# Attention weights turned by VectorE block transposes and transfers within SBUF, with 512-column value products

## The chip, the core and the metric

The kernel runs on one core of a Trainium2 chip. A core has a matrix engine (TensorE, PE in the profile, with PEld for its weight loads), VectorE (DVE), ScalarE (ACT), GpSimd (POOL) and SyncE (SP, which here only issues transfers), and 16 DMA engines that all queues share. On chip, data lie in SBUF (128 partitions); TensorE writes to PSUM. The metric is the device time of one execution in microseconds (us); lower is better. Each engine takes its own instructions strictly in the order in which the built program has them, and waits at an instruction until what it needs is there.

## What is computed

One layer with two parallel branches over 512 tokens of width 2048. In the attention branch there are 8 query heads of width 128 and 2 key/value heads. Cut to what matters:

```python
h = rms_norm(x, norm_w)
proj = jnp.einsum('bsd,de->bse', h, w_in)
q, k, v, g_attn, xr, g_lru = jnp.split(proj, SPLITS, axis=-1)
# attention_group, after norm and rope of q and k; 8 heads, 512 queries, 512 keys
s = jnp.einsum('bkgqd,bksd->bkgqs', q, k_t) * scale
p = jax.nn.softmax(s, axis=-1)
attn = jnp.einsum('bkgqs,bksd->bkgqd', p, v_t)
# lru_group: conv, two gated linear scans
mixed = concat([rms_norm(attn, attn_norm_w) * silu(g_attn),
                rms_norm(lru, lru_norm_w) * silu(g_lru)])
return x + jnp.einsum('bse,ed->bsd', mixed, w_out)
```

The scores of a block come out with 128 queries on the partitions and 512 keys along the row, which is right for the softmax. The sum over keys needs the keys on the partitions, so each head's 512 by 512 weights have to be turned between the two products. All matrix products are made in three parts from a high and a low half of each operand (`mm3`, lines 147 to 150): high by high, high by low, low by high.

## The kernel before, in words

The stages follow each other: the projection of the LRU inputs (with x turned on the way), the LRU branch under further projections, the q, k, v projections, attention, then the gates and the output projection. The TensorE order is written by hand for the whole kernel (`manual_schedule(engines={PE})`, line 983). A long TensorE work that waits for little (`fill`, the projection of the gates in `gates()`, line 1090) is woven with the attention chain by `weave` (line 336): each `yield n` of the chain lets n pieces of the fill follow, a piece being six 128x512 products. The other engines and the transfer queue of SyncE are ordered, for this stage, by a planner when the program is built; weight loads are asked for early (`high_priority(AHEAD)`, line 217) and go through a ring of three SBUF places (`wring`). A load thus waits until the VectorE split that last read its place is done (line 213). The split halves of a weight tile have four places each (`wh`, `wl`, line 210), two tiles to a load.

The attention stage (`attention`, line 624) has 32 steps, four blocks of 128 queries for each of eight heads:

- `weights` (line 581): three score products into a PSUM bank (`mm`, four banks), the row maximum on VectorE (line 588), the exponential with its row sum on ScalarE (591), the reciprocal on VectorE (592), and the scaling by it on GpSimd (593).
- `turn_weights` (line 596), two steps later: four 128x128 TensorE transposes into a PSUM bank (line 600), the high half by ScalarE (602), the low half by VectorE (603).
- `values` (line 605), for two blocks at once, three steps after the second of them began: twelve products of 256 columns into a bank, a VectorE copy out of it (615), and once a head a square on ScalarE and its sum on GpSimd.
- `turned` (line 573): the queries of a later head are turned on TensorE (541) and split. Two heads are held.
- After each step, `yield STEPS` lets two pieces of fill go. One transfer of `last_sums` (line 765), which adds up blocks of w_out in DRAM for the output stage, is also put in: adds on GpSimd's queue (750), copies on SyncE's (747).

The gates of the LRU branch are applied in `gate` (line 648), which writes the silu of a gate to working tiles of the attention pool and multiplies by it on VectorE.

Of the kernel before, what the change touches and what calls it, by code (L numbers as in the profile page):

```python
# [10 lines left out]
F32 = mybir.dt.float32  # L11
# [5 lines left out]
P = 128  # L17
# [13 lines left out]


LRU_K2, LRU_B4 = 12, 9
ATT_K2, ATT_B4 = 9, 9


AHEAD = 600
# [5 lines left out]
WARM, WARM2 = 14, 5  # L43


STEPS = 2


H = 256


C_Q, C_K, C_GA, C_XR, C_GL = 0, 1024, 1536, 2560, 3584
# [6 lines left out]
def hybrid_kernel(  # L59
# [51 lines left out]
    def nm(s):  # L111
        cnt[0] += 1
        return f"{s}_{cnt[0]}"
# [1 line left out]
    def x2():  # L115
        return pools["xw"].tile([P, SEQ], F32R, tag="x2", bufs=32, name=nm("x2"))

    def work():
        return ("lru", LRU_K2, LRU_B4) if "lru" in pools else ("att", ATT_K2, ATT_B4)

    def k2(dt=F32, shape=(P, SEQ)):
        pool, n, _ = work()
        return pools[pool].tile(list(shape), dt, tag="k2", bufs=n, name=nm("k2"))

    def b4(dt=F32, shape=(P, 2, SEQ)):
        pool, _, n = work()
        return pools[pool].tile(list(shape), dt, tag="b4", bufs=n, name=nm("b4"))

    def ev(dt=F32):

# [441 lines left out]

    def turned(rot, h):

        q = b4(F32R)
        split_ps(turn(rot, h), q[:, 0, :], q[:, 1, :])
        return q[:, 0, :], q[:, 1, :]

    last_scale = [None]

    def weights(q, g, t):

        qh, ql = q
        tt = slice(t * P, (t + 1) * P)
        sc = mm()
        mm3(sc, qh[:, tt], ql[:, tt], kth[g], ktl[g], True, True)
        mx = pools["att"].tile([P, 1], F32, tag="mx", bufs=6, name=nm("mx"))
        nc.vector.tensor_reduce(mx, sc, axis=AX.X, op=ALU.max, negate=True)  # L588
        p = k2()
        sm = pools["att"].tile([P, 1], F32, tag="sm", bufs=6, name=nm("sm"))  # L590
        nc.scalar.activation(p, sc, AF.Exp, bias=mx, accum_out=sm)
        nc.vector.reciprocal(sm, sm)
        last_scale[0] = nc.gpsimd.tensor_scalar(p, p, sm, 0.0, op0=ALU.mult, op1=ALU.add).ins
        return p

    def turn_weights(p, t, pth, ptl):
        tt = slice(t % 2 * P, (t % 2 + 1) * P)
        pt = mm()
        for s in range(NT):
            nc.tensor.transpose(pt[:, s * P : (s + 1) * P], p[:, s * P : (s + 1) * P], ident)  # L600
# [4 lines left out]
    def values(h, half, pth, ptl):  # L605

        gs = slice(h // G * HD, (h // G + 1) * HD)
        o = mm()[:, : 2 * P]
        for s in range(NT):
            mm3(o, vh[s][:, gs], vl[s][:, gs], pth[:, s, :], ptl[:, s, :], s == 0, s == NT - 1)  # L610
        if half == 0 and h % 2 == 0:
            ap_[h // 2] = aring.tile([P, 2, SEQ], F32, name=nm("av"))
        av, asum = ap_[h // 2][:, h % 2, :], sums["a"]
        to = slice(half * 2 * P, (half + 1) * 2 * P)
        nc.vector.tensor_copy(av[:, to], o)
        if half == 1:
            if h == 0:
                nc.scalar.activation(asum, av, AF.Square)
            else:
                sq = k2()  # L620
                nc.scalar.activation(sq, av, AF.Square)
                nc.gpsimd.tensor_add(asum, asum, sq)
# [24 lines left out]

    def gate(gs, pairs, row, sig):

        for e, g in enumerate(gs):  # L650
            if e == 0 or sig is not k2:
                ss = [sig() for _ in gs] if sig is k2 else [sig()]
                for s, src in zip(ss, gs if sig is k2 else [g]):
                    nc.scalar.activation(s, src, AF.Silu)
            s = ss[e] if sig is k2 else ss[0]
# [434 lines left out]
    def gates():  # L1090
        todo = iter(())
        for n, (c0, row) in enumerate(((C_GL, R_LN), (C_GL + SEQ, R_LN + 4), (C_GA, R_AN))):
# [6 lines left out]
                wait -= 1  # L1099
                yield  # L1100
            if n < 2:
                todo = gate(evac_bc(acc), hp[2 * n : 2 * n + 2], row, k2)
            else:
                late.extend(evac_bc(acc))

# [121 lines left out]
```

## Time and profile before

| | |
|---|---|
| median of 3 runs | 654.27 us (654.11 to 654.38) |
| span of the profiled execution | 652.6 us, 8664 instructions |
| attention stage (first to last row maximum on VectorE) | 275.4 to 417.9 us |
| TensorE busy | 646.9 us, 99% |
| VectorE, ScalarE, GpSimd busy | 475.7, 341.4, 101.2 us |

Only the span of the profiled execution is recorded. Beside the median of the unprofiled runs it leaves some 1.7 us for what lies around the span. In the profile, "busy" counts an instruction from its start to its modelled end; matmuls are pipelined, so a 128x512 product that shows 389 ns can be followed by the next after 227 ns. What a product costs is therefore read from the distance between starts, or from the chain of work that ended last, which gives each piece only the time by which it moved the end. A row of the timeline has the start in us, the duration in us, the engine, the line in the code and the operation, and in brackets how long the engine had stood idle before it and who released it.

### The profile page before, as it was taken

The page shows a single profiled execution, that of the slowest core. Times are in us where ns is not written, and L with a number is a line of the kernel's source. Part 1 is how long each engine was busy: PE and PEld are TensorE (multiplying, and loading weights), DVE is VectorE, ACT ScalarE, POOL GpSimd, SP SyncE. Part 2 cuts the span into 40 slices and gives each one's busy share as a digit, 9 for nine tenths or more (in the row PEclk, how much of TensorE's full clock was granted, in tenths as well). Part 3 has the DMA queues.
Part 4 walks back from the last instruction along what each step waited for, and adds up shares of the span by engine and source line. Part 5 has one row for each costly group of instructions (what it writes and reads, how often), then busy time and mean ns, then how long its engine had stood idle before and what let it go on. Part 6 is the DMA issues. An engine that isn't in the chain of part 4 may idle for free.

```text
span 652.6 us, 8664 instructions
## 1 busy us (share of the span) xinstructions
PE 646.9 (99%) x3059; PEld 538.9 (83%) x3059; DVE 475.7 (73%) x780; ACT 341.4 (52%) x598; POOL 101.2 (16%) x137
## 2 busy tenths in 40 slices
PE   9999999999999999999999999999999999999997
PEld 7888888888888888888888888888888888888885
DVE  5889689977688953855856567579837867797785
ACT  3534899489856515454744437454434554444441
POOL 0000101112013302142222434300000001020010
PEclk9999999999999999999999999999999999999999
DMA  9854685856468331467422575532336585798262
GB/s 291 281 143 127 142 207 152 207 139 152 140 198 255 100 93 33 124 129 187 109 66 54 123 128 115 91 105 74 116 101 204 180 292 179 283 318 274 76 194 96
DMA packets 56316, 102.48 MB, mean 157 GB/s; under 512 B 4696, under 2 KB 15056, under 8 KB 56272
## 3 DMA queue, kind: packets, MB, share of 16 engines
q1 hardware_dynamic: 48240, 84.09, 40.4%
q0 software_dynamic: 7712, 17.31, 15.6%
q10 hardware_dynamic: 320, 0.53, 0.3%
q8 instruction: 24, 0.39, 0.2%
q14 instruction: 20, 0.16, 0.1%
HBM read 97.71 MB, written 25.17 MB: 188 GB/s over the span
## 4 chain that ended last, share of the span: by engine, by line
PE 99%; DVE 0%; DVEq 0%; issue 0%; POOL 0%; POOLq 0%
PE pj L148 20%; PE pj L150 20%; PE pj L149 20%; PE mm L874 13%; PE pj L874 10%; PE mm L148 3%; PE mm L150 3%; PE mm L149 3%; PE mm L600 2%; PE mm L238 1%; PE pj L304 1%; PE mm L541 1%; PE mm L990 1%; PE mm L667 0%; PE mm L284 0%; DVE cb L905 0%
## 5 line engine op out<-in xcount | busy, mean ns | idle before, releaser
L148 PE MATMUL pj<-x,wh 128*128 128x512 f32 x376 | 149.1, 396 | 0.0
L150 PE MATMUL pj<-x,wl 128*128 128x512 f32 x376 | 147.0, 391 | 0.0
L149 PE MATMUL pj<-x,wh 128*128 128x512 f32 x376 | 146.4, 389 | 0.0
L212 ACT CAST wh<-wr 128x512 fp32r<-128x512 f32 x143 | 86.1, 618 | 80.3 <-PE pj L149 31.0
L213 DVE TENSOR_TENSOR wl<-wr,wh 128x512 fp32r<-128x512 f32 x144 | 101.6, 728 | 33.7 <-ACT wh L212 25.5
L725 ACT CAST wh<-wr 128x1024 fp32r<-128x1024 f32 (+1 forms) x72 | 60.6, 860 | 75.2 <-PE mm L874 37.2
L726 DVE TENSOR_TENSOR wl<-wr,wh 128x1024 fp32r<-128x1024 f32 (+1 forms) x72 | 68.6, 984 | 25.3 <-ACT wh L725 25.1
L150 PEld LDWEIGHTS pj<-x,wl 128*128 128x128 f32 x376 | 70.6, 188 | 15.2
L149 PEld LDWEIGHTS pj<-x,wh 128*128 128x128 f32 x376 | 70.7, 188 | 13.6
L148 PEld LDWEIGHTS pj<-x,wh 128*128 128x128 f32 x376 | 70.6, 188 | 13.3
L148 PE MATMUL pj<-wh,x 128*128 128x512 f32 x192 | 74.9, 390 | 0.0
L150 PE MATMUL pj<-wh,x 128*128 128x512 f32 x192 | 74.7, 389 | 0.0
L149 PE MATMUL pj<-wl,x 128*128 128x512 f32 x192 | 74.7, 389 | 0.0
L602 ACT CAST b<-mm 128x512 fp32r<-128x512 f32 x32 | 18.8, 586 | 62.2 <-PE mm L600 62.2
L874 PE MATMUL mm<-wh,ml 128*128 128x512 f32 x128 | 49.8, 389 | 0.0
L874 PE MATMUL mm<-wh,mh 128*128 128x512 f32 x128 | 49.8, 389 | 0.0
L874 PE MATMUL mm<-wl,mh 128*128 128x512 f32 x128 | 49.8, 389 | 0.0
L750 POOL DMA_DIRECT2D t<-in_w_out_dram x40 | 33.1, 838 | 102.0 <-DMA t<-in_w_out_dram 101.8
L588 DVE TENSOR_REDUCE mx<-mm 128x1 f32<-128x512 f32 x32 | 22.1, 690 | 33.4 <-PE mm L150 32.6
L150 PEld LDWEIGHTS pj<-wh,x 128*128 128x128 f32 x192 | 36.0, 188 | 7.6
L148 PEld LDWEIGHTS pj<-wh,x 128*128 128x128 f32 x192 | 36.1, 188 | 7.4
L149 PEld LDWEIGHTS pj<-wl,x 128*128 128x128 f32 x192 | 36.1, 188 | 7.3
(205 smaller groups left out, 1115.8 us busy)
## 6 DMA issues: line engine op xcount, KB each, us to landing
wr<-in_w_in_dram SPq DMA_DIRECT2D x71, 512.0 KB, 3.9
wr<-in_w_out_dram SPq DMA_DIRECT2D x24, 512.0 KB, 4.9
t<-in_w_out_dram POOLq DMA_DIRECT2D x40, 256.0 KB, 5.8
wr<-t SPq DMA_DIRECT2D x40, 256.0 KB, 4.2
t<-in_w_out_dram SPq DMA_DIRECT2D x24, 256.0 KB, 4.8
t<-t SPq DMA_DIRECT2D x16, 256.0 KB, 4.0
wr<-in_w_out_dram SPq DMA_DIRECT2D x16, 256.0 KB, 5.1
wr<-in_x_dram POOLq DMA_DIRECT2D x8, 512.0 KB, 5.8
```

The source lines that it names most:

```text
L148: nc.tensor.matmul(acc, lh, rh, start=start, stop=False)
L149: nc.tensor.matmul(acc, lh, rl, start=False, stop=False)
L150: nc.tensor.matmul(acc, ll, rh, start=False, stop=stop)
L212: copy(hi, raw[:, k, :])
L213: nc.vector.tensor_sub(lo, raw[:, k, :], f(hi))
L588: nc.vector.tensor_reduce(mx, sc, axis=AX.X, op=ALU.max, negate=True)
L600: nc.tensor.transpose(pt[:, s * P : (s + 1) * P], p[:, s * P : (s + 1) * P], ident)
L602: nc.scalar.copy(pth[:, :, tt], p3)
L725: nc.scalar.copy(hi[:, to], b)
L726: nc.vector.tensor_sub(lo[:, to], b, f(hi[:, to]))
L750: nc.gpsimd.dma_start(dst, src, accum_op=ALU.add)
L874: nc.tensor.matmul(dst[s], lh[:, ts_], rh, start=i == 0 and j == 0, stop=i == 7 and j == 2)
```

## The change

Per head, instead of per two blocks:

- each scaled weight block is turned by a VectorE instruction that transposes every 32x32 square by itself (line 594 of the changed kernel), into a tile `u` (two of them);
- `moved` (596): after the fourth block, 16 transfers on SyncE's queue carry the squares of a head to their partitions, from `u` into one tile `pt`, in pieces of 512 bytes, 32 partitions and 64 KB a transfer (602); then ScalarE makes the high half and VectorE the low half in two instructions each of 128x1024 (607, 608), into one pair `ph`, `pl`;
- `values` (611) makes twelve products of 512 columns a head, and the copy out of the bank (620) puts the columns back in order. It stands directly behind the score products of the fourth block of the next head;
- the TensorE transposes and the PSUM banks they took are gone; one head's queries are turned ahead instead of two;
- the silu of a gate is written in place (line 658), so that the attention pool needs no tiles for it; the fill gets 13 + 36 x 2 pieces within the chain instead of 13 + 35 x 2, and the rest follows as before.

```diff
-    def weights(q, g, t):
+    def weights(q, g, t, turned_):
...
         last_scale[0] = nc.gpsimd.tensor_scalar(p, p, sm, 0.0, op0=ALU.mult, op1=ALU.add).ins
-        return p
-
-    def turn_weights(p, t, pth, ptl):
-        tt = slice(t % 2 * P, (t % 2 + 1) * P)
-        pt = mm()
+        nc.vector.transpose(turned_[:, :, t, :], p)
+
+    def moved(turned_):
+
+        u = turned_.rearrange("p (s a) t c -> p a s (t c)", a=NQ)
+        pt = at("pt", 1, (NT, NQ, P))
+        for i in range(NQ):
+            for a in range(NQ):
+                nc.sync.dma_start(pt[a * B : (a + 1) * B, :, i, :], u[i * B : (i + 1) * B, a])
+        hi, lo = at("ph", 1, (NT, SEQ), F32R), at("pl", 1, (NT, SEQ), F32R)
+        p = pt.rearrange("p s i x -> p s (i x)")
+        for s in range(0, NT, 2):
+            ss = slice(s, s + 2)
+            nc.scalar.copy(hi[:, ss], p[:, ss])
+            nc.vector.tensor_sub(lo[:, ss], p[:, ss], f(hi[:, ss]))
+        return hi, lo
+
+    def values(h, hi, lo):
+
+        gs = slice(h // G * HD, (h // G + 1) * HD)
+        o = mm()
         for s in range(NT):
-            nc.tensor.transpose(pt[:, s * P : (s + 1) * P], p[:, s * P : (s + 1) * P], ident)
-        p3 = pt.rearrange("p (s q) -> p s q", q=P)
-        nc.scalar.copy(pth[:, :, tt], p3)
-        nc.vector.tensor_sub(ptl[:, :, tt], p3, f(pth[:, :, tt]))
...
-            mm3(o, vh[s][:, gs], vl[s][:, gs], pth[:, s, :], ptl[:, s, :], s == 0, s == NT - 1)
+            mm3(o, vh[s][:, gs], vl[s][:, gs], hi[:, s], lo[:, s], s == 0, s == NT - 1)
...
-        nc.vector.tensor_copy(av[:, to], o)
+        nc.vector.tensor_copy(
+            av.rearrange("p (t i c) -> p i t c", i=NQ, c=B),
+            o.rearrange("p (i t c) -> p i t c", i=NQ, c=B),
+        )
...
-        qs, ps_, pts = {h: turned(rots[0], h) for h in range(2)}, {}, {}
-        yield 13
+        qs, pts = {h: turned(rots[0], h) for h in range(1)}, {}
+        yield BEGIN
         last = NH * NT
-        for i in range(last + 3):
+        for i in range(last + NT):
             h, t = divmod(i, NT)
             if i < last:
-                ps_[i] = weights(qs[h], h // G, t)
+                if t == 0:
+                    u = at("u", 2, (SEQ // B, NT, B))
+                weights(qs[h], h // G, t, u)
                 next(transfers, None)
-                if t == 0 and h + 2 < NH:
-                    qs[h + 2] = turned(rots[(h + 2) // G], (h + 2) % G)
-            j = i - 2
-            if 0 <= j < last:
-                h, t = divmod(j, NT)
-                if t % 2 == 0:
-                    pts[j // 2] = b4(F32R, (P, NT, 2 * P)), b4(F32R, (P, NT, 2 * P))
-                turn_weights(ps_.pop(j), t, *pts[j // 2])
-            j = i - 3
-            if j >= 0 and j % 2 == 1:
-                values(j // NT, j // 2 % 2, *pts.pop(j // 2))
+                if t == 0 and h + 1 < NH:
+                    qs[h + 1] = turned(rots[(h + 1) // G], (h + 1) % G)
+                if t == NT - 1:
+                    pts[h] = moved(u)
+            if t == NT - 1 and h:
+                values(h - 1, *pts.pop(h - 1))
             yield STEPS
...
-            if e == 0 or sig is not k2:
-                ss = [sig() for _ in gs] if sig is k2 else [sig()]
-                for s, src in zip(ss, gs if sig is k2 else [g]):
+            if e == 0 or sig:
+                ss = [sig()] if sig else gs
+                for s, src in zip(ss, [g] if sig else gs):
                     nc.scalar.activation(s, src, AF.Silu)
```

More of the change, by code (lines that the diff above doesn't have):

```diff
@@ L43 @@
 WARM, WARM2 = 14, 5
-STEPS = 2
+BEGIN, STEPS = 13, 2
 H = 256
+B = 32
+NQ = P // B
 C_Q, C_K, C_GA, C_XR, C_GL = 0, 1024, 1536, 2560, 3584
@@ L116, in x2, with at @@
         return pools["xw"].tile([P, SEQ], F32R, tag="x2", bufs=32, name=nm("x2"))
-    def work():
-        return ("lru", LRU_K2, LRU_B4) if "lru" in pools else ("att", ATT_K2, ATT_B4)
     def k2(dt=F32, shape=(P, SEQ)):
-        pool, n, _ = work()
-        return pools[pool].tile(list(shape), dt, tag="k2", bufs=n, name=nm("k2"))
+        return pools["lru"].tile(list(shape), dt, tag="k2", bufs=LRU_K2, name=nm("k2"))
     def b4(dt=F32, shape=(P, 2, SEQ)):
-        pool, _, n = work()
-        return pools[pool].tile(list(shape), dt, tag="b4", bufs=n, name=nm("b4"))
+        return pools["lru"].tile(list(shape), dt, tag="b4", bufs=LRU_B4, name=nm("b4"))
+    def at(tag, bufs, shape, dt=F32):
+        return pools["att"].tile([P, *shape], dt, tag=tag, bufs=bufs, name=nm(tag))
     def ev(dt=F32):
@@ L586, in weights @@
         mm3(sc, qh[:, tt], ql[:, tt], kth[g], ktl[g], True, True)
-        mx = pools["att"].tile([P, 1], F32, tag="mx", bufs=6, name=nm("mx"))
+        mx, sm = (at(n, 6, (1,)) for n in ("mx", "sm"))
         nc.vector.tensor_reduce(mx, sc, axis=AX.X, op=ALU.max, negate=True)
-        p = k2()
-        sm = pools["att"].tile([P, 1], F32, tag="sm", bufs=6, name=nm("sm"))
+        p = at("p", 3, (SEQ,))
         nc.scalar.activation(p, sc, AF.Exp, bias=mx, accum_out=sm)
@@ L605, in values @@
[L605 to L609, printed above, removed]
-            mm3(o, vh[s][:, gs], vl[s][:, gs], pth[:, s, :], ptl[:, s, :], s == 0, s == NT - 1)
-        if half == 0 and h % 2 == 0:
+        nc.vector.transpose(turned_[:, :, t, :], p)
[12 more added lines that the diff above has]
+        return hi, lo
@@ L1101, in gates @@
             if n < 2:
-                todo = gate(evac_bc(acc), hp[2 * n : 2 * n + 2], row, k2)
+                todo = gate(evac_bc(acc), hp[2 * n : 2 * n + 2], row, None)
             else:
```

20 lines of the change are left out of this document (9 added, 11 removed).

## The prediction

> **What bounds the kernel now.** I read the page first (busy shares, then the chain that ended last), then the chain in order of time inside the attention stage, then the timeline of one attention step, then SyncE's waits and the transfer table, and last the granted clock.
>
> ```profile
> span 652.6 us, 8664 instructions
> PE 646.9 (99%) x3059; PEld 538.9 (83%) x3059; DVE 475.7 (73%) x780; ACT 341.4 (52%) x598; POOL 101.2 (16%) x137
> PE 99%; DVE 0%; DVEq 0%; issue 0%; POOL 0%; POOLq 0%
> ```
>
> TensorE is never without work: the chain is TensorE for 99% of the span. So what leaves TensorE's program shortens the kernel one for one, and every wait that is put into that program lengthens it one for one. Here is the attention stage on that chain (start, time on the chain, what):
>
> ```profile
> 299.99 0.24 PE mm L150
> 300.23 0.44 PE mm L600 x4
> 300.67 0.12 PE mm L148
> 300.78 0.12 PE mm L149
> ...
> 301.97 0.12 PE mm L150
> 302.08 0.23 PE pj L148
> ```
>
> Four turns cost 0.44 us, the twelve value products of 256 columns 302.08 - 300.67 = 1.41 us, and a 512-column product 0.23 us (0.227 in long rows).
>
> **What leaves TensorE.** The line of the turns, and the copy that stands once behind each set of value products:
>
> ```profile
> L600 PE MATMUL mm<-ident,k x128: 270/272/273, 282.6 to 425.8; 128*128 128x128 f32 x128
> L615 DVE COPY av<-mm x16: 404/416/426, 293.4 to 430.3; 128x256 f32<-128x256 f32 x16
> ```
>
> 128 turns are 32 groups: 32 x 0.44 = 14.1 us. Value products: 16 x 1.41 = 22.6 us become 8 x 12 x 0.227 = 21.8 us, so 0.8 us. The turns of the queries stay eight. Together 14.9 us off TensorE, if nothing waits.
>
> **What is added, and the wait it brings.** The changed kernel's built order decides here. For heads 2 and 3 it has (numbers tell tiles apart; u_3194 is head 3, pl_3149 and ph_3148 are head 2):
>
> ```
> TensorE   mm_3289 <- kt, q        three score products, head 3, fourth block
>           mm_3325 <- ph_3148      value products of head 2: high half
>           mm_3325 <- pl_3149      low half, the second of the twelve
> VectorE   mx_3293 (maximum), sm_3294 (reciprocal), u_3194 <- p_3296 (turn)   head 3, fourth block
>           pl_3149 <- pt_3131, ph_3148   twice, head 2
>           av_3338 <- mm_3325
> ```
>
> On TensorE the value products of head 2 stand directly behind the last scores of head 3. On VectorE their low half stands behind the turn of the block made from those same scores. So the second value product cannot start before scores, maximum, exponential, reciprocal, scaling, turn and split have run one after the other, and TensorE has nothing else to take. This is so at seven places (heads 0 to 6); at head 1 the low half stands behind the turn of the third block and the maximum of the fourth instead. One step of before gives the links:
>
> ```profile
> 299.83 0.40 PE L150 MATMUL mm<-kt,b 128*128 128x512 f32 x1
> 300.27 0.69 DVE L588 TENSOR_REDUCE mx<-mm 128x1 f32<-128x512 f32 x1
> 301.19 0.69 ACT L591 ACTIVATE k<-mm,mx 128x512 f32<-128x512 f32 x1
> 301.77 0.20 ACT L591 ACTIVATION_READ_ACCUMULATOR k<-mm,mx 128x1 f32 x1
> 302.00 0.16 DVE L592 RECIPROCAL sm<-sm 128x1 f32<-128x1 f32 x1
> 302.26 0.69 POOL L593 TENSOR_SCALAR k<-k,sm 128x512 f32<-128x512 f32 x1 [1.86 <-DVE sm L592]
> L726 DVE TENSOR_TENSOR wl<-wr,wh 128x1024 fp32r<-128x1024 f32 x40 | 48.6, 1223 | 20.0 <-ACT wh L725 19.8
> L725 ACT CAST wh<-wr 128x1024 fp32r<-128x1024 f32 x40 | 41.7, 1052 | 60.7 <-PE mm L874 35.6 <-DVE wr L827 11.1 <-PE pj L874 4.0
> ```
>
> From the start of the last score product: the maximum starts at 0.44 and ends at 1.13; the exponential can follow at 1.19 (here it came later, ScalarE was busy); from its start to the end of the scaling are 302.95 - 301.19 = 1.76, so 2.95. The turn has no row. Below it I put the 128x256 copy (0.42), above it the 128x1024 subtraction (1.22); I take 0.69, VectorE's 128x512 maximum, the same shape and type: 0.08 to start, 3.72. The first low half (128x1024 in SBUF, as line 726): 0.06 + 1.22, 5.00; TensorE goes on at 5.05. Unhindered, the second value product would start after two products, at 0.46. The wait is 4.6 us (4.3 to 5.1 with the ends for the turn). The second low half takes 1.2 us more and is hidden by the six products of the first (1.36 us). ScalarE's high half (1.05 us) runs while VectorE and GpSimd finish the block. VectorE itself gains per head four turns (2.8 us) and loses little; in
>
> ```profile
> 305.00:325.00 20.00, 20.00 (x113) 17.08 (x112) 15.63 (x28) 13.18 (x25) 3.91 (x6) 1.00 0.53 136
> 325.00:345.00 20.00, 20.00 (x111) 17.03 (x110) 11.74 (x22) 9.42 (x21) 5.02 (x6) 1.00 0.18 54
> ```
>
> (stretch; sum; then PE, PEld, DVE, ACT, POOL, clock, DMA share, GB/s) it is busy 15.6 and 11.7 of 20 us; a head will last over 21 us, so its amount of work isn't the bound, its order is. The weight splits behind the values (next chunk) are needed three fill pieces and more later, 4 us; hidden.
>
> [...]
>
> **The transfers.** They have one head's time, less what precedes. Rows:
>
> ```profile
> SPq L201 <- DVE wl L213: 309.1, 53, 12.9
> wr<-in_w_in_dram SPq DMA_DIRECT2D x71, 512.0 KB, 3.9
> k<-in_lru_wa_dram SPq DMA_DIRECT2D x8, 128.0 KB, 3.8
> k<-in_lru_wx_dram SPq DMA_DIRECT2D x8, 128.0 KB, 4.8
> 42.51 2.00 SPq L393 DMA_DIRECT2D k<-in_lru_wa_dram  x4
> 44.55 2.00 SPq L394 DMA_DIRECT2D k<-in_lru_wx_dram  x4
> DMA to landing us min/median/max: 3.6/4.8/6.1
> out_dram<-cb SPq DMA_DIRECT2D x3, 256.0 KB, 2.5
> out_dram<-cb POOLq DMA_DIRECT2D x4, 256.0 KB, 8.3
> L750 POOL DMA_DIRECT2D t<-in_w_out_dram x40 | 33.1, 838 | 102.0 <-DMA t<-in_w_out_dram 101.8
> ```
>
> An issue takes 0.5 us, and loads in 512-byte pieces (those of the LRU gate maps, eight of 128 KB: 1 MB, as much as a head's weights) land 3.8 to 4.8 us after it, at most 6.1. The 16 transfers of head 2 cannot start before the split of head 1 has left `pt`, which is when TensorE goes on at values 1 (time 0 now). In SyncE's order two weight loads stand among them (four, a load, six, a load, four), and a weight load waits until VectorE has split the tile that held its place: SyncE waits for that 309 us in all today, up to 12.9 us at once, and the last four transfers will wait behind it. The second load's place comes free after value products (2.5), two fill pieces (2.7), scores and turn (1.1), two pieces (2.7), scores (0.7), one piece (1.4), a cast (0.6), and a low half behind the reciprocal (1.3) that shares VectorE: 13.4 with the links' gaps. Four issues later, 15.3, plus 3.8 landing: 19.1; high half 1.1, low half 1.3, TensorE at 21.6. The chain of the fourth block ends at 16.9 us of TensorE work (4 x 0.7 scores, 0.44, 8 x 1.36, 2.7) plus 4.6, at 21.5. The two are even. If the transfers land 1 us later (4.8), each wait is 1 us longer; at 6.1, 2.3 us. If they land at 2.5, the lower end, from the fastest row of this queue above, the block's chain decides and nothing is gained. I take 4.8 us a wait: 7 x 4.8 = 33.6 us.
>
> Head 7 has no scores beside it: from values 6 TensorE has 2.5 + 8 x 1.36 = 13.4 us, and two loads stand among its transfers too, the second free at about 6.6; four issues and 3.8 land at 12.4, with both halves 14.8: 1 us of wait (0 to 3).
>
> SBUF writes of 8 MB more share the 16 DMA engines, busy 0.53 and 0.18 of those stretches: the weight loads, issued some 10 us ahead, cover that; uncovered, it is inside the 2.3 us above. The adds on GpSimd follow the scaling as before (0.8 us between blocks 3.4 us apart). Gates in place: the same instructions, free of charge; the tiles are in time, as a gate's projection takes over 60 us.
>
> **The clock.** A TensorE that stands still for over 4 us is something this trace shows only at its end:
>
> ```profile
> 1.13 3.17 PE mm L990 x14
> 5.56 1.07 PE mm L990 x5
> 6.62 1.17 PE pj L304 x4
> 647.59 0.39 PE L874 MATMUL mm<-wh,ml 128*128 128x512 f32 x1
> 650.00:651.00 1.00, 0.00 (x0) 0.00 (x0) 0.00 (x0) 0.00 (x0) 0.00 (x0) 1.00 0.43 128
> 651.00:652.00 1.00, 0.00 (x0) 0.00 (x0) 0.00 (x0) 0.00 (x0) 0.00 (x0) 0.96 0.00 0
> 652.00:652.60 0.60, 0.00 (x0) 0.00 (x0) 0.00 (x0) 0.00 (x0) 0.00 (x0) 0.50 0.00 0
> ```
>
> The granted clock (the third number from the right) falls to half at 651.92, 3.9 us after the last product ended. At the start (the first three rows, of the chain) a product of 256 columns takes 3.17 / 14 = 0.226 us, twice the 0.12 us above: half speed after standing still. Those at 5.56 still take 0.21; the four of 512 columns from 6.62 take 0.29 each, between 0.23 and its double, so full speed came back near 6.8, some 5.7 us after the first product. So gaps of 4.4 us (TensorE's first value product, with the high half, runs before the wait) may halve the clock in some heads. I take two of seven, since the gap is little longer than the 3.9 us, and 5.7 us at half rate after each, half of it lost: 2 x 2.8 = 5.7 us; ends 0 and 7 x 2.8 = 20 us. [...]
>
> **The sum.** -14.9 + 33.6 + 1 + 5.7 = +25.4 us. The profiled span of 652.6 leaves 1.7 us around it to the median of 654.27; both carry over. 654.3 + 25.4 = 679.7.
>
> **Rivals.**
> - Nothing waits (the other side): the low half of a head is ready before the scores of the next end, as its transfers would allow only if VectorE held it ahead of the fourth block's turn. 654.3 - 14.9 = 639.4. It decides where the wait falls under 14.9 / 7 = 2.1 us; maximum, exponential, scaling and split alone are 3.3. For it speaks only that TensorE's amount falls. 0.03.
> - The clock never falls: the gaps stay too short for it, as only one is seen to do so. 654.3 - 14.9 + 34.6 = 674. 0.24.
> - The clock falls in every gap: 654.3 - 14.9 + 34.6 + 20 = 694; for it speaks that the one gap seen did. 0.16.
> - The transfers are the bound: 32 partitions at a time, SBUF at both ends, no row shows it. At the 8.3 us of the outputs on GpSimd's queue the wait is 4.7 + 8.3 - 3.8 = 9.2 us: 654.3 - 14.9 + 64 + 4 (head 7), and with the clock down in each gap 20 more: 727. Against it: 512-byte pieces landed in 3.8. 0.12.
>
> **How the numbers follow.** My forecast has 0.45. Predicted 679.7. Range 668 (waits of 4.2 us, no clock fall) to 702 (waits of 5.5, all clocks): it holds the first, third and fourth case and leaves out some 0.2. A difference under 0.2% (1.3 us) cannot be told here; faster 0.03, same 0.01, slower 0.96.
>
> **What would show it.** TensorE idle in seven places of 4 to 6 us between 300 and 450 us, just ahead of products that read `pl`, released by VectorE's low half; no line of turns by `ident` on the weights; VectorE's turn near 0.69 us; the last transfer of a head landing close to the end of the next head's scaling; granted clock 1.00, or 0.50 behind some gaps. The prediction is wrong if VectorE's low half runs before the fourth turn, if the waits are released by transfers and far longer, or if TensorE also waits for weight splits (`wl`).

## The result and the profile after

The changed kernel takes 706.92 us (705.73 to 707.14) against 654.19 us beside it: 1.080 times as long, 95% interval 1.0785 to 1.0816. The forecast had 679.7 us, range 668 to 702: slower, as forecast, but by 52.7 us where 25.4 were given.

The page of the changed kernel: the span, busy shares, and the rows of TensorE's busy tenths and granted clock over 40 slices of 17.6 us.

```profile
span 704.9 us, 8366 instructions
PE 654.6 (93%) x2835; PEld 533.0 (76%) x2835; DVE 493.1 (70%) x788; ACT 346.0 (49%) x586; POOL 101.3 (14%) x137
...
PE   9999999999999999938977877797999999999997
...
PEclk9999999999999999969888978989999999999999
...
PE 77%; issue 6%; DMA 6%; DVE 4%; POOL 3%; ACT 2%; SPq 1%; DVEq 0%; ACTq 0%; POOLq 0%
```

TensorE was 99% of the chain before and is 77% now, and its holes lie in the attention slices alone (the last slice is the program's end), as do the clock's digits under 9. Who ended the holes, from the changed kernel's waits (us in total, times, longest):

```profile
PE mm L149 <- ACT ph L607: 38.2, 8, 11.5
PE mm L150 <- DVE pl L608: 6.3, 8, 1.4
```

That is 44.5 us in eight places. What the clock took is in the same kernel's windows, one for each stretch at half rate (length, TensorE busy, four other engines, clock, DMA share, GB/s):

```profile
303.18:316.83 13.65, 5.09 (x11) 3.71 (x12) 2.36 (x2) 1.99 (x2) 0.02 (x1) 0.50 0.79 215
...
357.79:364.61 6.82, 5.72 (x13) 4.15 (x14) 2.95 (x3) 0.89 (x1) 0.00 (x0) 0.50 0.16 39
...
sum 61.44, PE 40.27 PEld 29.45 DVE 22.38 ACT 11.47 POOL 4.73; mean PE 5.03 PEld 3.68 DVE 2.80 ACT 1.43 POOL 0.59
```

Eight stretches, one behind each gap, in which TensorE worked 40.3 us at half rate; at full rate, taking the granted 0.50 for half the pace, that is 20.1 us less (a product follows the one before after 0.43 us at 385.62 to 388.18, after 0.23 at 389.95 to 391.54). So: -14.9 (work that left TensorE) + 44.5 + 20.1 = 49.7 of the 52.3 us by which the span grew. The other 2.6 us lie in TensorE's work: at full rate it is 634.5 us (654.6 - 20.1), which is 12.4 less than the 646.9 of before, not 14.9.

Where a head's time goes shows on SyncE's timeline for the transfers of head 3, counted from 0 (start, length of the run of issues, line), and then on all engines where the fourth block of head 4 meets the value products of head 3:

```profile
360.78 4.45 SPq L602 DMA_DIRECT2D pt<-u  x7
368.34 0.37 SPq L202 DMA_DIRECT2D wr<-in_w_in_dram  x1
368.76 5.10 SPq L602 DMA_DIRECT2D pt<-u  x8
375.50 0.37 SPq L202 DMA_DIRECT2D wr<-in_w_in_dram  x1
375.92 0.59 SPq L602 DMA_DIRECT2D pt<-u  x1
```

```profile
378.12 0.40 PE L149 MATMUL mm<-kt,q 128*128 128x512 f32 x1
...
381.74 0.71 DVE L594 STREAM_TRANSPOSE u<-p 128x512 f32<-128x512 f32 x1 [0.82 <-POOL p L593]
382.25 1.99 ACT L607 CAST ph<-pt 128x1024 fp32r<-128x1024 f32 x2 [1.52 <-DMA pt<-u]
383.32 2.36 DVE L608 TENSOR_TENSOR pl<-pt,ph 128x1024 fp32r<-128x1024 f32 x2 [0.87 <-ACT ph L607]
383.34 0.79 PE L149 MATMUL mm<-ph,v 128*128 128x512 f32 x1 [4.35 <-ACT ph L607]
384.60 0.79 PE L150 MATMUL mm<-pl,v 128*128 128x512 f32 x1 [0.47 <-DVE pl L608]
```

The transfers' last landing (382.2) and the fourth block's turn (382.45) do end level. But the first value product waits too, for the high half, which needs only the transfers. (At heads 1 and 2 the high half follows the exponential on ScalarE without a pause, at 332.56 and 356.68 us, so there ScalarE's order ended the wait; at the other six it was a transfer.) And the transfers form a round: from 360.78, when the split of head 2 has left `pt`, 16 issues take 10.1 us, SyncE stands 3.1 and 1.6 us in front of two weight loads whose ring place is not free, and the 16th transfer lands late. Its time to landing is in the transfer table (last number, median), for the windows 360 to 368, 368.7 to 374.5 and 374 to 384 us:

```profile
pt<-u SPq DMA_DIRECT2D x7, 64.0 KB, 2.0
...
pt<-u SPq DMA_DIRECT2D x8, 64.0 KB, 3.4
...
pt<-u SPq DMA_DIRECT2D x1, 64.0 KB, 6.1
```

The median is 2.0 us for seven transfers with no load ahead and 3.4 for eight behind a 512 KB load and beside a w_out add; the one behind the second load, with two w_out adds beside it, took 6.1. (The first load had landed by then, at 372.6.) What makes the later ones slower these rows do not show; in a run below, with no load among the transfers, the medians of two heads are 2.0 us and, with w_out adds running among them, 3.8.

Head 0 is the worst, 12.0 us of waits. On SyncE's timeline, three copies for the output stage stand ahead of its transfers and wait for GpSimd's adds:

```profile
283.67 8.18 SPq L751 DMA_DIRECT2D t<-t  x3
...
292.53 8.17 SPq L602 DMA_DIRECT2D pt<-u  x8
...
301.38 5.87 SPq L602 DMA_DIRECT2D pt<-u  x8
```

### The profile page after: what moved, and what is told of

Its sections match the earlier page's. It is cut to its first block, busy times and chain, and to the rows that moved or that the text cites. A ratio compares the mean times of both kernels' runs of the same rounds, so it can differ in the third digit from the quotient of the medians.

```text
span 704.9 us, 8366 instructions
## 1 busy us (share of the span) xinstructions
PE 654.6 (93%) x2835; PEld 533.0 (76%) x2835; DVE 493.1 (70%) x788; ACT 346.0 (49%) x586; POOL 101.3 (14%) x137
## 4 chain that ended last, share of the span: by engine, by line
PE 77%; issue 6%; DMA 6%; DVE 4%; POOL 3%; ACT 2%; SPq 1%; DVEq 0%; ACTq 0%; POOLq 0%
PE pj L149 14%; PE pj L150 14%; PE pj L151 14%; PE mm L878 12%; PE pj L878 9%; PE mm L150 4%; PE mm L151 3%; PE mm L149 3%; DMA pt<-u 3%; DMA wr<-in_w_in_dram 2%; DVE pl L608 1%; POOL p L593 1%; PE mm L239 1%; DVE wl L214 1%; DMA t<-in_w_out_dram 1%
## 5 line engine op out<-in xcount | busy, mean ns | idle before, releaser
L214 DVE TENSOR_TENSOR wl<-wr,wh 128x512 fp32r<-128x512 f32 x144 | 103.2, 742 | 41.3 <-ACT wh L213 30.3
L149 PEld LDWEIGHTS pj<-x,wh 128*128 128x128 f32 x376 | 71.1, 189 | 14.8
L150 PEld LDWEIGHTS pj<-x,wh 128*128 128x128 f32 x376 | 71.0, 189 | 14.9
L151 PEld LDWEIGHTS pj<-x,wl 128*128 128x128 f32 x376 | 70.7, 188 | 15.1
L149 PE MATMUL mm<-ph,v 128*128 128x512 f32 x32 | 20.6, 645 | 38.2 <-ACT ph L607 38.2
L149 PEld LDWEIGHTS mm<-ph,v 128*128 128x128 f32 x32 | 9.9, 309 | 43.9 <-ACT ph L607 41.7
```

Of the source, the lines that this page charges most:

```text
L149: nc.tensor.matmul(acc, lh, rh, start=start, stop=False)
L150: nc.tensor.matmul(acc, lh, rl, start=False, stop=False)
L151: nc.tensor.matmul(acc, ll, rh, start=False, stop=stop)
L214: nc.vector.tensor_sub(lo, raw[:, k, :], f(hi))
```

## The experiments

All times are medians, with the ratio to the kernel before on the same chip. "High" and "low" are TensorE's waits for `ph` and `pl`, in us, in the profiled run; "half rate" is TensorE's busy time at a clock of 0.5. The profiled execution is one of those timed, and in two rows it lies well above the median: 673.9 us for 669.0 and 658.8 for 654.4. In the column of loads, "among" means that SyncE has weight loads between a head's transfers.

| run | tiles | values later by | loads | us | ratio (95%) | high, low | half rate |
|---|---|---|---|---|---|---|---|
| changed kernel | 1 | 0 | among | 706.9 | 1.080 (1.0785-1.0816) | 38.2, 6.3 | 40.3 |
| filler products | 1 | 0 | among | 700.3 | 1.071 (1.0677-1.0743) | 14.2, 5.3 | 15.2 |
| no transfers | - | 0 | - | 642.1 | 0.981 (0.9797-0.9826) | 0, 0 | 0 |
| halves first | 1 | 0 | among | 716.2 | 1.093 (1.0894-1.0956) | 49.0, 3.7 | 43.2 |
| values later | 1 | 1 | among | 705.0 | 1.077 (1.0754-1.0789) | 38.0, 5.3 | 40.7 |
| two queues | 1 | 0 | among | 687.3 | 1.050 (1.0478-1.0529) | 17.6, 6.4 | 32.3 |
| two tiles | 2 | 0 | among | 688.7 | 1.052 (1.0506-1.0542) | 35.1, 1.4 | 17.9 |
| two tiles, later | 2 | 1 | among | 682.0 | 1.041 (1.0384-1.0435) | 27.8, 0.9 | 20.5 |
| two tiles, later still | 2 | 2 | among | 669.0 | 1.023 (1.0173-1.0279) | 14.1, 3.7 | 26.0 |
| loads behind | 1 | 0 | behind | 684.9 | 1.045 (1.0427-1.0477) | 20.9, 8.0 | 26.9 |
| four wide transfers | 1 | 0 | among | 667.2 | 1.020 (1.0175-1.0221) | 15.1, 4.0 | 14.8 |
| later, two queues | 2 | 2 | among | 679.2 | 1.037 (1.0356-1.0391) | 7.9, 3.8 | 14.4 |
| later, loads behind | 2 | 2 | behind | 654.4 | 1.000 (0.9983-1.0013) | 5.1, 1.1 | 15.9 |
| one tile, later, loads behind | 1 | 1 | behind | 670.3 | 1.023 (1.0188-1.0272) | 10.4, 10.0 | 17.5 |

**Is the clock a cause of its own?** 34 products of 256 columns (put at 4.0 us, 3.7 in the trace) stand ahead of each head's value products, in the bank that these then clear.

```diff
         o = mm()
+        for _ in range(FILLER):
+            nc.tensor.matmul(o[:, : 2 * P], wv[:, :P], wv, start=True, stop=True)
```

> The changed kernel with 34 idle products of 128x256 (0.118 us each, 4.0 us in all) in front of each head's value products, into the same bank, so that TensorE stands still for less than 2 us at a time. Theory (the waits of 44.5 us in eight places halve the clock eight times, 40.3 us of work at half rate, 20 us lost): the clock stays at 1.00, the waits are filled but not shortened, about 687 us (685 to 693, since the shortest waits of 3.5 us are overfilled by half a us). Rival (the half clock costs nothing, as the transfers set the pace of a head): 707 us or a little more.

700.32 us. Work at half rate falls from 40.3 to 15.2 us, which is worth 12.5 us, but the time only by 6.6: what is left of the waits (19.5 us) and the 29.8 us of filler are 4.8 us more than the 44.5 us of waits before. TensorE at full speed reaches its wait sooner, and the transfers come when they come. The clock is part of the price, not its root.

**Are the transfers the root?** They are left out, and the halves made from the turned tile directly, so the weights are in the wrong rows.

```diff
-        for i in range(NQ):
-            for a in range(NQ):
-                nc.sync.dma_start(pt[...], u[...])
...
-        p = pt.rearrange("p s i x -> p s (i x)")
+        p = turned_.rearrange("p n t c -> p (n t c)").rearrange("p (s e) -> p s e", s=NT)
```

> The changed kernel without the 128 transfers: the halves are made from the tile that VectorE's turns have written, so the weights are in the wrong order and the value products are of other sums; all engines' work is the same. Theory (turns and splits on VectorE fit in, the wait comes with the transfers and the order they give): no waits, 639 to 642 us. Rival (VectorE's added turns or the one head's delay cost by themselves): over 650 us.

642.09 us, no wait for either half, clock full: the expectation holds. The turns, halves and 512-column products by themselves gain 12.3 us; the transfers cost 64.8.

**Is it the order on VectorE?** Once with the maximum and exponential of a fourth block ordered behind the halves of the head before, once with the value products a step (two fill pieces and a block of scores) later.

```diff
+        with behind(last_lo, t):
             nc.vector.tensor_reduce(mx, sc, axis=AX.X, op=ALU.max, negate=True)
...
+        with behind(last_hi, t):
             nc.scalar.activation(p, sc, AF.Exp, bias=mx, accum_out=sm)
```

> The changed kernel with one edit of order: on VectorE the maximum of a head's fourth block comes behind the low half of the head before, and on ScalarE its exponential behind the high half; so the halves no longer stand behind the fourth block's chain. Theory (two bounds that are about even, the chain of the fourth block and the transfers; the transfers of a head now begin one block's chain, some 3 us, later): waits as long or longer, now all released by transfers, 700 to 725 us. Rival (the order on VectorE alone makes the wait): waits fall to 1 us or less and the clock stays up, 642 to 652 us.

716.22 us, slower, as the theory had it: the halves wait for the transfers, and now the block waits behind the halves. Nearly all of its waits are for `ph` (49.0 us). Order alone is not the cause.

```diff
-BEGIN, STEPS = 13, 2
+BEGIN, STEPS = 11, 2
...
-            if t == NT - 1 and h:
-                values(h - 1, *pts.pop(h - 1))
+            hv, tv = divmod(i - 1, NT)
+            if tv == NT - 1 and hv > 0:
+                values(hv - 1, *pts.pop(hv - 1))
```

> The changed kernel with the value products one step (two pieces of fill, some 3.9 us with scores and a turn) later in TensorE's program. In the built order the low half again stands behind the turn of the block whose scores come just ahead of the value products. Theory (order): each wait stays near 4.2 us, the extra of the heads that waited for transfers (head 0: 7 us, heads 3, 4, 6: some 1 us, head 7: 4 us) goes, clock falls remain: 685 to 697 us. Rival (only the transfers are late): waits fall to under 1 us, 642 to 652 us.

704.99 us; both expectations fell. A step of work put in front of the value products bought next to nothing: head 0's wait fell from 12.0 to 8.0 us, and in sum the waits (38.0 and 5.3 us) are what they were. A round explains that. A head's halves begin when its transfers have landed, and the next head's transfers begin when these halves have left `pt`. In this run the low half of head 2 ended at 357.25, the transfers of head 3 began at 357.27 and the last of them landed at 378.90; head 3's high half began at 379.07, its low half ended at 382.51, and the next transfers began at 382.54. That is 25.3 us from start to start (24.9 in the changed kernel, 360.78 to 385.71), and the value products are no direct link of it (TensorE enters only through the weight loads among the transfers, which wait for a place). While the round is longer than TensorE's own work for a head, TensorE waits for the difference wherever they stand. The next runs take the round into their theories.

**Which link of the round?** First the issue: eight of a head's transfers go to ScalarE's queue. Then the tile: the low half is written over the transferred weights, and there are two such tiles, so that transfers need not wait for the split of the head before.

```diff
-                nc.sync.dma_start(pt[...], u[...])
+                (nc.sync, nc.scalar)[a % 2].dma_start(pt[...], u[...])
```

> Edit: of a head's 16 transfers eight are issued by ScalarE's queue and eight by SyncE's; one tile pt as in the changed kernel. Theory A (two bounds that stand level: the chain of the fourth block, and the round through the one tile pt): the transfers land some 4 us earlier (8 issues of 0.6 us less, weight loads in front of fewer), the chain of the fourth block stays, so the wait for the high half shrinks to under 2 us, that for the low half grows to 2 to 4 us, and the time is 692 to 706. Rival B (the round through pt alone sets the pace): every head is 4 to 5 us shorter, and with fewer falls of the clock 655 to 675. Rival C (what the transfers cost is their landing and the contention of the DMA engines, not their issue): nothing changes, 703 to 710.

687.34 us, between the two expectations: 20 us off, so issue and what stands between the issues weigh far more than "level" allows, and less than all. A new wait comes with it, 4.6 us for `p`: the exponentials queue behind ScalarE's issues.

```diff
-        pt = at("pt", 1, (NT, NQ, P))
+        pl = at("pl", 2, (NT, NQ, P), F32R)
+        pt = f(pl)
```

> Edit: the transferred weights and their low half share one tile, and there are two of these, so that the transfers of a head start behind its own fourth turn and no longer wait for the split of the head before. The order on TensorE and VectorE is as in the changed kernel. Theory A: the chain of the fourth block stays; no wait for the high half (under 0.5 us), a wait for the low half of 3 to 5 us in most heads, 675 to 695 with the clock's falls. Rival B (the round through pt alone): the waits go, 640 to 655. Rival C (the transfers as such, whatever tile they go to): waits for the high half stay, 700 to 710.

688.65 us lies in the range of theory A, and for the wrong reason. A's wait for the low half (3 to 5 us) is not there. The wait is for the high half, at every second head only. From the waits and, for one such head, the timeline:

```profile
PE mm L149 <- ACT ph L608: 35.1, 4, 11.3
PE mm L150 <- DVE pl L609: 1.4, 3, 0.5
```

```profile
379.11 1.90 SPq L603 DMA_DIRECT2D pl<-u  x3
381.11 0.54 SPq L202 DMA_DIRECT2D wr<-in_w_in_dram  x1
381.69 5.74 SPq L603 DMA_DIRECT2D pl<-u  x8
388.49 0.37 SPq L202 DMA_DIRECT2D wr<-in_w_in_dram  x1
388.91 13.62 SPq L603 DMA_DIRECT2D pl<-u  x16
```

```profile
397.68 1.99 ACT L608 CAST ph<-pl 128x1024 fp32r<-128x1024 f32 x2 [3.97 <-DMA pl<-u]
```

A head's transfers now start right behind its own fourth turn, at 379.1, with two loads among them, and the last lands near 397.7: 18.6 us. TensorE has some 13 us of work from that turn to the value products, so it waits 6.8 us; during that wait the next head's fourth turn is done, its transfers get a start of their own, and it doesn't wait. With the round broken, the transfers' own length is the bound.

The next two give them more time, with the first maximum and exponential of a head kept behind the halves of the head before the last (in the runs three steps later below, the second).

> Edit: two tiles as in the run before; the value products of a head stand behind the first scores of the head after the next instead of the last of the next, and the first maximum and exponential of a head stand behind the halves of the head before the last, so that nothing of the first block's chain stands ahead of them on VectorE and ScalarE. Theory A: both bounds are gone; the transfers have one head's 17 us less the two weight loads that SyncE waits for, 14 us are needed (16 issues of 0.6, one or two waits, 3 to landing): waits of 0 to 2 us, 640 to 655. Rival C: 700 to 710.

> Edit: as the run before, with the value products one more step later (behind the second scores). Theory A: 4 us more for the transfers than there; no waits but at the first and last head, clock at 1.00: 639 to 648, about 2 to 5 us of it the end of the last head, faster than both kernels. Rival C (transfers as such): 690 to 710.

682.03 and 669.04 us: better with each step, and both above what A gave. The waits left are for the high half (27.8 and 14.1 us), behind loads on SyncE. Two tiles and time are not enough while loads stand among the transfers.

**The weight loads.** The changed kernel with one tile; the planner is told to put a head's transfers first.

```diff
-                nc.sync.dma_start(pt[...], u[...])
+                with tc.high_priority(AHEAD):
+                    nc.sync.dma_start(pt[...], u[...])
```

> Edit: the changed kernel with its one tile; only SyncE's order differs: a head's 16 transfers stand together, and the weight loads that stood among them (with their wait for a place) stand behind. Theory A (the round through the one tile is as long as its issues, the waits of SyncE for the places of weight loads, the landing and the halves): some 3 to 5 us a head less in front of the last transfer, so that the chain of the fourth block is left: high half's wait under 2 us in most heads, 685 to 698, like the run with two queues (687). Rival B (the loads' waits lie beside the transfers' own pace and cost nothing): 703 to 710. Rival D (the loads come too late for TensorE's fill pieces when they stand behind): a new wait on wh or wl, 700 or more.

684.88 us, 0.1 below theory A's range; rivals B and D fall (no wait on `wh` or `wl` in attention). SyncE's timeline for head 3 and the transfer table (353 to 372 us):

```profile
355.70 10.26 SPq L603 DMA_DIRECT2D pt<-u  x16
366.06 5.29 SPq L202 DMA_DIRECT2D wr<-in_w_in_dram  x2
```

```profile
pt<-u SPq DMA_DIRECT2D x16, 64.0 KB, 2.0
```

All sixteen are out in 10.3 us and land after 2.0. The next head's, with w_out adds running among them and the loads again behind, land later (372 to 392 us):

```profile
t<-in_w_out_dram POOLq DMA_DIRECT2D x4, 256.0 KB, 5.3
pt<-u SPq DMA_DIRECT2D x16, 64.0 KB, 3.8
```

The last of these landed at 394.71 after 4.8 us, 0.36 us behind an add that landed at 394.35. What stays is head 0's wait (11.3 us), in six others 1.2 to 4.1, and none at head 7. At head 4, one of the longest of these, the chain of the fourth block is laid bare, on all engines:

```profile
392.63 0.40 PE L151 MATMUL mm<-kt,q 128*128 128x512 f32 x1
...
393.97 0.69 ACT L591 ACTIVATE p<-mm,mx 128x512 f32<-128x512 f32 x1 [2.40 <-DVE mx L589]
...
394.88 1.99 ACT L608 CAST ph<-pt 128x1024 fp32r<-128x1024 f32 x2
...
395.77 0.71 DVE L594 STREAM_TRANSPOSE u<-p 128x512 f32<-128x512 f32 x1 [0.82 <-POOL p L593]
...
395.98 0.50 PE L149 MATMUL mm<-ph,v 128*128 128x512 f32 x1 [2.96 <-ACT ph L608]
396.40 2.32 DVE L609 TENSOR_TENSOR pl<-pt,ph 128x1024 fp32r<-128x1024 f32 x2
...
397.64 0.50 PE L150 MATMUL mm<-pl,v 128*128 128x512 f32 x1 [1.16 <-DVE pl L609]
```

The high half stands behind the fourth exponential on ScalarE, the low half behind the fourth turn on VectorE, and nothing waits for a transfer, if only just at this head: 5.0 us from the start of the last score product to TensorE's going on with the low half (397.64). Heads 2 and 6 wait as long (4.1 us), and there the last transfer had been issued 2.1 and 7.1 us before the high half began. The order is thus a second bound, which shows when the transfers are out of the way.

Next, four transfers of 256 KB over all partitions (weights in the wrong rows), as many bytes:

```diff
-            for a in range(NQ):
-                nc.sync.dma_start(pt[a * B : (a + 1) * B, :, i, :], u[i * B : (i + 1) * B, a])
+            nc.sync.dma_start(pt[:, :, i, :], u[:, i])
```

> Edit: four transfers of 256 KB over all 128 partitions a head (no change of partition, so the weights stand in the wrong rows) in place of sixteen of 64 KB; as many bytes, the same 512-byte pieces, one tile. Theory A: 12 issues of 0.6 us less are 7 us; the chain of the fourth block is left, 680 to 695. Rival E (bytes or pieces set the transfers' pace, not the count of issues): the issues and landings grow in step, 700 to 710. The planner also moves the low half a few places earlier on VectorE here, which can take some us off.

667.16 us, better than the theory's 680 and against rival E, though landing doubles (median 6.1 us against 3.0). So the bytes alone are not the price. The count of issues is the likely one, but the transfers also keep their partitions here, fewer loads stand among them, and the planner's order on VectorE is another; these were not separated.

**All together.** Two tiles and values two steps later, once with two queues, once with the loads behind.

> Edit: two tiles and the value products two steps later (669 in that run, where the waits that were left were for the high half, 14 us, behind weight loads on SyncE's queue), and eight of a head's 16 transfers on ScalarE's queue. Theory A: the last transfer is 5 us and more earlier: no wait but at head 0 (up to 6 us, where the copies of w_out stand ahead on SyncE), 640 to 652. Rival F (ScalarE's queue holds up the exponentials, 8 issues of 0.6 to 0.8 us a head): waits on p or ph, 655 to 675.

> Edit: two tiles and the value products two steps later, and SyncE's weight loads behind a head's transfers instead of among them. Theory A: no wait for the high half but at head 0 (under 3 us, the transfers go ahead of the copies there too), 640 to 650, faster than both kernels. Rival D (the loads come too late): waits on wh or wl, 655 to 690. Rival B: 665 to 672 as before.

679.16 and 654.43 us. With ScalarE issuing, rival F's mechanism comes, stronger than its range: 10 us slower than without it. From its waits:

```profile
PE mm L149 <- ACT p L600: 11.9, 5, 3.3
```

With the loads behind, the time is that of the kernel before (0.9998, 0.9983 to 1.0013), 4 us above the expectation. In the profiled execution, the longest of ten (652.9 to 658.8), two heads still wait for transfers (6.2 us), the first scores 1.8 us for their queries, and 15.9 us of work run at half rate.

> Edit: one tile as in the changed kernel; value products one step later (705 when done alone) and the weight loads behind a head's transfers (685 when done alone). Theory G (the round through the one tile, about 16 issues of 0.7, 3 to land, 2.3 for the halves: 17 us and whatever queues in front of the halves on ScalarE and VectorE, is as long as TensorE's 16.9 us a head): waits of 1 to 3 us a head stay, 660 to 680. Rival H (one tile is enough once the loads are out of the way): 645 to 657.

670.30 us, as theory G has it: one tile, with the loads behind and the value products one step later (not two), leaves some 20 us of waits, spread over the heads.

**Is the work that left TensorE ever had?** With two tiles, loads behind and an earlier fill:

> Edit: the version that gave 654.4 (two tiles, values two steps later, loads behind), with two fill pieces more ahead of the first scores (two fewer at the end). Theory: the 1.8 us in which the first scores wait for the first queries, and the fall of the clock behind it (1.7 us), go; the rest stays: 650 to 652.5. Rival: the last head now waits at the end, 653 to 657.

> Edit: two tiles, loads behind, values three steps later, fill pieces ahead as in the version of 654.4. Theory: 4 us more for the transfers: the waits at head 0 (3.6 us) and at the one late head (2.6 us) and the clock's falls behind them (6.3 us) go, the first scores' 3.5 us stay: 641 to 648. Rival: the tail of the last head or the halves' place on ScalarE and VectorE brings new waits: 650 to 660.

> Edit: as the run before with two fill pieces more ahead of the first scores (and four fewer at the end). Theory: nothing waits but a little at the end: 639 to 645, 1.5 to 2.3% faster than before. Rival: new waits at the end of the last head (3 to 6 us and a fall of the clock): 645 to 655.

659.03, 655.96 and 652.95 us; none as low as its theory. In the first the scores' wait went, as expected, but another head's transfers came 7.6 us late, not the last one's. The third is the first to beat the kernel before, by 0.4% (0.996, 0.994 to 0.9981). Its longest wait, 2.7 us, is for `p`; the next run was to remove it, and the last one drops the added order altogether.

> Edit: the version of 653 with the halves of a head ahead of the third maximum and exponential of the head after the next (not the second). Theory: the 2.7 us wait for p at head 0 and the fall behind it (1.7 us) go, the rest stays: 646 to 650. Rival: the halves now end later than the value products want them, waits on ph and pl of 1 to 3 us in several heads: 653 to 665.

> Edit: the version of 653 without the added order of halves and maxima; the planner's own. Theory: with two tiles and values three steps later the halves have time enough whatever the planner does: 646 to 653. Rival: the planner puts the low half behind a turn in front of the values again, waits on pl of 1 to 4 us a head: 655 to 675.

652.92 and 651.82 us (0.9965, 0.9951 to 0.9979; 0.9947, 0.9931 to 0.9964). The last lies in its theory's range and is the fastest here, without any added order:

```diff
-BEGIN, STEPS = 13, 2
+BEGIN, STEPS = 11, 2
...
-        pt = at("pt", 1, (NT, NQ, P))
+        pl = at("pl", 2, (NT, NQ, P), F32R)
+        pt = f(pl)
...
+                with tc.high_priority(AHEAD):
+                    nc.sync.dma_start(pt[...], u[...])
...
+            hv, tv = divmod(i - 3, NT)
...
-            yield STEPS
+            yield STEPS - (last <= i < last + 4)
```

The wait for `p` stayed in both (2.1 and 2.4 us), so the added order was not its cause. In the last run's waits and on ScalarE's timeline:

```profile
PE mm L149 <- ACT p L591: 2.4, 1, 2.4
```

```profile
306.54 1.05 ACT L609 CAST ph<-pl 128x1024 fp32r<-128x1024 f32 x1 [7.46 <-DMA wr<-in_w_in_dram]
...
309.48 0.68 ACT L591 ACTIVATE p<-mm,mx 128x512 f32<-128x512 f32 x1
```

ScalarE stands 7.5 us at the first high half of head 0, and the exponential queued behind it is late. The profile names a weight load issued right behind the transfers. But the high half reads `pl`, which the transfers write and the load does not; the last of head 0's sixteen was issued at 300.60 us. So that transfer itself seems to have landed late, some 5.9 us after its issue (2.0 to 6.9 for this run's transfers, median 3.6). No load stood among these transfers; a w_out add on GpSimd's queue was in flight (300.02 to 306.20 us). So the adds, which no run moved, are a rival to SyncE's queue as the cause of late landings, and what is left to try.

Of the 14.9 us that were to leave, 2.8 are had (654.63 - 651.82). Some 8.5 us of waits are left in the profiled run, 2.3 of them for the high half of a weight, now that loads come behind the transfers, and 1.7 us of clock.

## Why the prediction was wrong

By its own steps. Two failed most: the place of the wait (the high half, behind the transfers, not the low half) and the clock's term (5.7 us given, 20.1 measured).

- **What leaves TensorE, 14.9 us: nearly right.** Without transfers TensorE is busy 13.5 us less than before (633.4 against 646.9) and idle for 1.4, and the time is 642.1 against 654.4.
- **The turn, 0.69 us: right,** 0.71 measured (the turn's row in the timeline above).
- **4.8 us a wait for heads 1 to 6: right in sum by luck, wrong in place.** Measured 28.2 us against 28.8. "TensorE's first value product, with the high half, runs before the wait" failed: that product is what waits (38.2 of 44.5 us), for the transfers at six heads, and where these are early (heads 1 and 2, and the run with the loads behind) for the high half's turn on ScalarE behind an exponential.
- **The chain of the fourth block: there, but not first.** It was put at 5.05 us from the start of the last score product to TensorE's going on; with the loads behind it shows at 5.0.
- **The transfers' terms.** The last issue was put to end 15.3 us behind the split; it ended 15.7 us behind (376.51 - 360.78). Issue 0.5, measured 0.60. The landing, 3.8 for all, came to 6.1 for the one that counts at head 3. Weight loads "among them" were priced as a wait for a place; that transfers with loads and adds in flight also land later (3.4 and 6.1 us beside 2.0) was not. So the high half began 21.5 us behind the split where 19.1 were given. The split was also taken to be done when TensorE goes on, but TensorE goes on behind its first half (359.67) and the transfers begin behind the second, 1.1 us later. That the two ends still came level (382.2 and 382.45) is in part luck: the half-rate stretch before (357.79 to 364.61, 5.72 us of work) had put the block off by 2.9 us too. That a faster transfer gains little beside an even chain did not hold: the loads moved behind gained 22.0 us, 15.6 of them waits, 6.7 the clock.
- **Head 0 (4.8 us) and head 7 (1.0): too small,** 12.0 and 4.3 measured, 10.5 us together. The copies of w_out in front of head 0's transfers on SyncE's queue were not counted.
- **The clock, 5.7 us: the largest miss.** Two gaps of seven were taken "since the gap is little longer than the 3.9 us"; all eight brought a fall, 20.1 us. The rival in which it falls in every gap (694, given 0.16) was the nearest; with heads 0 and 7 as measured it makes 704.5. The rival in which the transfers are the bound (727, given 0.12) had the releaser of six of the eight high-half waits right, and its landing of 8.3 us too long.
- **What was taken to be hidden was:** TensorE waits for no weight split in the stage, and VectorE's amount of work is not the bound.

## What to carry to other kernels

A transfer put between two steps of a pipeline is to be costed as a round: issue time by count (0.60 us each here), everything else in its queue (and what that waits for), landing beside the other traffic in flight (2.0 to 6.1 us at head 3), the work that frees its tile. Of the remedies tried alone that keep the result, none gave more than 22 us of the 52.7; two tiles, later use and a queue without loads together gave 52.5. Where such a round leaves TensorE idle, nearly half as much again can go with its clock (20.1 beside 44.5 us here), so a forecast of waits needs one of the clock beside it.

## What the runs showed of the hardware

**The clock fell behind stretches that were up to 39% busy.** In the changed kernel TensorE is busy for 0.00 to 1.33 of the 3.41 us (the length of its shortest stretch at half rate) ahead of each of the eight falls in attention, and for 3.28 us or more of the 3.41 ahead of each return to 1.00. The busiest of those ahead of a fall is the one that ends at 333.90 us; its row and the next ones:

```profile
330.49:333.90 3.41, 1.33 (x6) 0.73 (x4) 2.59 (x6) 3.38 (x6) 0.69 (x1) 1.00 0.22 86
333.90:340.73 6.83, 5.44 (x13) 4.04 (x13) 3.60 (x5) 1.32 (x3) 0.69 (x1) 0.50 0.08 19
340.73:344.14 3.41, 3.41 (x16) 2.72 (x16) 2.50 (x3) 1.66 (x3) 1.29 (x1) 1.00 0.16 38
```

From 473.85 to 477.26 us TensorE is busy for 1.70 us, and the clock stays at 1.00 there and in the 3.41 us behind it. In the fastest run, of two waits of about the same length, 2.4 us at 307.89 and 2.3 at 357.99, only the first brings a fall: TensorE is busy for 1.22 us in the row of the first, and for 2.10 and 2.44 us in the two rows into which the second falls.

```profile
308.11:311.52 3.41, 1.22 (x4) 0.86 (x5) 3.41 (x5) 3.39 (x6) 0.00 (x0) 1.00 0.35 79
355.89:359.30 3.41, 2.10 (x12) 1.40 (x10) 2.21 (x3) 2.00 (x2) 0.26 (x1) 1.00 1.05 315
359.30:362.72 3.42, 2.44 (x9) 1.72 (x10) 1.76 (x4) 2.34 (x5) 0.00 (x0) 1.00 0.83 211
```

So the length of a wait alone did not tell in that run whether the clock would fall. The prediction took the 3.9 us of a standstill as the mark, and so the four-us gaps for a toss-up.
